# Setting the single_packet flag on SyncE's loads and stores in a rotary-embedding score kernel

## Chip, cores and metric

The kernel runs on one core of one Trainium2 chip. The metric is the device time of one execution in microseconds. A run counts as fast when it is within 1.5% of the fastest run of the same kernel.

## The reference

```python
batch, seq, heads, dim = 16, 512, 16, 64          # q, k float32, [batch, seq, heads, dim]
q_rot = concat([q1*cos - q2*sin, q1*sin + q2*cos])  # halves of dim; the same for k
scores = np.einsum('bshd,bthd->bsht', q_rot, k_rot)  # float32, [16, 512, 16, 512]
```

The inputs are 67 MB, the output is 268 MB. Per batch and head there is one product of 512 x 64 by 64 x 512.

## The kernel before: the parts that matter

Rows of the sequence are dealt to 128 partitions, four (C = 4) to each. VectorE applies the rotation, TensorE transposes and multiplies, ScalarE copies the scores from PSUM into one of three stage buffers of 32 KB per partition (16 heads x 512 x 4 bytes), and SyncE issues the store. Every load and store goes through SyncE's ring; only the two small tables (cos, sin) are issued by ScalarE. A ring is the queue of transfers of one issuing engine; in the profile q1 is SyncE's, q10 ScalarE's, q0 GpSimd's. "Row" means a contiguous piece of memory per partition: 32 KB in a full store, 16 KB in a batch load. The cuts below have comments added.

```python
stage_pool = ctx.enter_context(tc.tile_pool(name="stage", bufs=3))
...
def load(which, b):                       # 30 of these: 128 rows of 16 KB, 2 MB
    ...
    nc.sync.dma_start(t.rearrange("p c (h d) -> p c h d", h=H), dram[which][b])
...
def store(i, st):                         # 59 of these: 128 rows of 32 KB, 4 MB
    o = o_v[i // C, i % C]
    if i < NST - 1:
        nc.sync.dma_start(o, st)
        return
    h = H - 2                             # the last store, in three pieces
    nc.sync.dma_start(o[:, :h], st[:, :h])
    nc.sync.dma_start(o[:116, h:], st[:116, h:])
    nc.sync.dma_start(o[116:, h:], st[116:, h:])
...
def scores(i, p, st):
    ...                                   # matmuls into ps
    nc.scalar.copy(out=so, in_=si)        # L173: st <- ps
    if b == 0 and p % 2 == 1:             # 16 of these: 128 rows of 8 KB, 1 MB
        nc.sync.dma_start(o_v[0, c, :, G * i : G * (i + 1)], st[:, G * c : G * (c + 1)])
```

## Time and profile before

| | before |
|---|---|
| time, median of the first 3 runs | 800.30 us (800.18 to 802.09) |
| span of the profiled execution | 799.0 us |
| moved | 336.17 MB, mean 421 GB/s |
| DMA engines busy with SyncE's ring | 98.6% of the span |

### The profile page before, as it was taken

Reading aid. Unit: us, or ns where it says so; the run is one execution under the profiler, and the core shown is the slowest. Engines: PE = TensorE matmul, PEld = TensorE weight load, DVE = VectorE, ACT = ScalarE, POOL = GpSimd, SP = SyncE. Lnnn points to the kernel's source line nnn. Section 1 sums busy time; section 2 is a strip of 40 time slices with the busy share of each in tenths; the row PEclk is TensorE's granted clock in tenths of the full one; section 3 lists DMA queues with packets and bytes.
Section 4 is the critical chain, followed back from the end, with each engine's and each line's share of the span. In section 5 each row is a group of like instructions: output and inputs, shape, how many; then the busy total and the mean of one; then the engine's idle time right before and its main releaser. Section 6 shows DMA issues by size and latency. Waiting matters only on the chain.

```text
span 799.0 us, 7715 instructions
## 1 busy us (share of the span) xinstructions
PE 691.3 (87%) x3072; PEld 299.3 (37%) x3072; DVE 544.6 (68%) x516; ACT 561.2 (70%) x647; POOL 0.7 (0%) x6
## 2 busy tenths in 40 slices
PE   4989998997979979799797997979979799799970
PEld 2444443343434334343343443424434343344420
DVE  6999987676866768577585775857758478585300
ACT  3888886775857758577585775757757677578870
POOL 0000000000000000000000000000000000000000
PEclk9999999898998989889898898988989899899995
DMA  9999999999999999999999999999999999998995
GB/s 355 422 424 424 432 427 433 425 435 427 421 437 426 439 427 430 433 431 430 431 428 433 434 428 429 433 438 420 418 426 434 435 415 418 426 440 375 422 439 231
DMA packets 17844, 336.17 MB, mean 421 GB/s; under 512 B 1808, under 2 KB 3088, under 8 KB 4240
## 3 DMA queue, kind: packets, MB, share of 16 engines
q1 hardware_dynamic: 17520, 335.55, 98.6%
q8 instruction: 24, 0.39, 0.2%
q10 hardware_dynamic: 288, 0.13, 0.1%
q14 instruction: 12, 0.10, 0.0%
HBM read 67.24 MB, written 268.44 MB: 420 GB/s over the span
## 4 chain that ended last, share of the span: by engine, by line
DMA 50%; PE 40%; ACT 4%; DVE 3%; issue 1%; ACTq 0%; SPq 0%; DVEq 0%
DMA out_dram<-st 47%; PE ps L166 30%; PE bank L127 10%; ACT st L173 4%; DMA q_sb<-in_q_dram 2%; DVE part L106 1%; DMA early<-in_k_dram 1%; DVE q_sb L107 0%; DVE k_sb L107 0%; DVE k_sb L111 0%; DVE q_sb L111 0%; DVE early L107 0%; DVE kT_t L142 0%; ACTq L281 0%; DVE early L111 0%
## 5 line engine op out<-in xcount | busy, mean ns | idle before, releaser
L173 ACT COPY st<-ps 128x1024 f32<-128x1024 f32 x512 | 494.7, 1018 | 203.7 <-DMA out_dram<-st 105.6
L166 PE MATMUL ps<-kT_t,qT_t 64*128 64x512 f32 x2048 | 548.9, 654 | 71.0 <-ACT st L173 70.9
L166 PEld LDWEIGHTS ps<-kT_t,qT_t 64*128 64x128 f32 x2048 | 185.0, 197 | 261.7 <-issue 144.6
L142 DVE COPY qT_t<-bank 128x512 f32<-128x512 f32 x118 | 81.6, 691 | 203.8 <-PE bank L127 203.8
L127 PEld LDWEIGHTS bank<-ident,q_sb 128*128 128x128 f32 x480 | 55.6, 152 | 102.5 <-issue 99.1
L127 PE MATMUL bank<-ident,q_sb 128*128 128x128 f32 x480 | 86.9, 308 | 0.9 <-PE ps L166 0.9
L127 PEld LDWEIGHTS bank<-ident,k_sb 128*128 128x128 f32 x480 | 50.5, 141 | 95.4 <-issue 38.7
L127 PE MATMUL bank<-ident,k_sb 128*128 128x128 f32 x480 | 78.7, 287 | 1.6 <-DVE qT_t L142 1.2
L142 ACT COPY kT_t<-bank 128x512 f32<-128x512 f32 x122 | 72.5, 599 | 6.4 <-PE bank L127 6.4
L107 DVE TENSOR_TENSOR q_sb<-q_sb,cos_t 128x1024 f32<-128x1024 f32 x60 | 73.5, 1226 | 2.1
L111 DVE TENSOR_TENSOR k_sb<-k_sb,part 128x1024 f32<-128x1024 f32 x60 | 73.5, 1225 | 2.1
L107 DVE TENSOR_TENSOR k_sb<-k_sb,cos_t 128x1024 f32<-128x1024 f32 x60 | 73.5, 1225 | 2.0
L106 DVE TENSOR_TENSOR part<-q_sb,ss_t 128x1024 f32<-128x1024 f32 x60 | 73.5, 1225 | 2.0
L106 DVE TENSOR_TENSOR part<-k_sb,ss_t 128x1024 f32<-128x1024 f32 x60 | 73.0, 1216 | 0.1
L111 DVE TENSOR_TENSOR q_sb<-q_sb,part 128x1024 f32<-128x1024 f32 x60 | 73.0, 1216 | 0.0
L127 PE MATMUL bank<-ident,early 128*128 128x128 f32 x64 | 10.5, 316 | 12.5 <-DVE early L111 10.6
L127 PEld LDWEIGHTS bank<-ident,early 128*128 128x128 f32 x64 | 8.3, 161 | 17.5 <-issue 13.4
L106 DVE TENSOR_TENSOR part<-early,ss_t 128x1024 f32<-128x1024 f32 x8 | 9.8, 1223 | 5.9 <-DMA early<-in_k_dram 5.8
L111 DVE TENSOR_TENSOR early<-early,part 128x512 f32<-128x512 f32 x16 | 10.3, 687 | 0.2
L107 DVE TENSOR_TENSOR early<-early,cos_t 128x1024 f32<-128x1024 f32 x8 | 9.8, 1225 | 0.3
L142 ACT COPY qT_t<-bank 128x512 f32<-128x512 f32 x10 | 5.7, 617 | 3.2 <-PE bank L127 3.2
L142 DVE COPY kT_t<-bank 128x512 f32<-128x512 f32 x6 | 4.1, 685 | 0.3 <-PE bank L127 0.3
(9 smaller groups left out, 2.8 us busy)
## 6 DMA issues: line engine op xcount, KB each, us to landing
out_dram<-st SPq DMA_DIRECT2D x59, 4096.0 KB, 23.9
k_sb<-in_k_dram SPq DMA_DIRECT2D x15, 2048.0 KB, 26.9
q_sb<-in_q_dram SPq DMA_DIRECT2D x15, 2048.0 KB, 29.9
out_dram<-st SPq DMA_DIRECT2D x16, 1024.0 KB, 14.3
out_dram<-st SPq DMA_DIRECT2D x1, 3584.0 KB, 20.4
early<-in_k_dram SPq DMA_DIRECT2D x1, 1536.0 KB, 8.9
early<-in_q_dram SPq DMA_DIRECT2D x1, 1536.0 KB, 12.1
early<-in_k_dram SPq DMA_DIRECT2D x1, 512.0 KB
```

The costliest lines, as they stand in the source:

```text
L106: nc.vector.tensor_tensor(pv, xs, ss, op=mult)
L107: nc.vector.tensor_tensor(xc, xc, cs, op=mult)
L111: nc.vector.tensor_tensor(y, y, z, op=add)
L127: nc.tensor.transpose(bank[:, x, :], src, ident)
L142: copy(out=dst, in_=src)
L166: nc.tensor.matmul(out=po, lhsT=lhs[64 * r : 64 * r + 64, :], rhs=rh, start=True, stop=True)
L173: nc.scalar.copy(out=so, in_=si)
```

## The change

The intent: let the descriptors of a transfer travel as one packet, so that the DMA engines pay less per row. The flag is set on 110 of SyncE's 112 transfers (the two odd pieces of the last store and ScalarE's two tables stay without it).

```diff
-        nc.sync.dma_start(t.rearrange("p c (h d) -> p c h d", d=D), src)
+        nc.sync.dma_start(t.rearrange("p c (h d) -> p c h d", d=D), src, single_packet=True)
...
-        nc.sync.dma_start(t.rearrange("p c (h d) -> p c h d", h=H), dram[which][b])
+        nc.sync.dma_start(t.rearrange("p c (h d) -> p c h d", h=H), dram[which][b], single_packet=True)
...
-            nc.sync.dma_start(o, st)
+            nc.sync.dma_start(o, st, single_packet=True)
...
-        nc.sync.dma_start(o[:, :h], st[:, :h])
+        nc.sync.dma_start(o[:, :h], st[:, :h], single_packet=True)
...
-            nc.sync.dma_start(o_v[0, c, :, G * i : G * (i + 1)], st[:, G * c : G * (c + 1)])
+            nc.sync.dma_start(o_v[0, c, :, G * i : G * (i + 1)], st[:, G * c : G * (c + 1)], single_packet=True)
```

## The prediction

> **What bounds the kernel now.** The first view read is the page's second and third part, because the change touches only transfers: the DMA row of the forty slices, the packet line, and the queues.
>
> ```profile
> DMA  9999999999999999999999999999999999998995
> ...
> DMA packets 17844, 336.17 MB, mean 421 GB/s; under 512 B 1808, under 2 KB 3088, under 8 KB 4240
> ## 3 DMA queue, kind: packets, MB, share of 16 engines
> q1 hardware_dynamic: 17520, 335.55, 98.6%
> ...
> q10 hardware_dynamic: 288, 0.13, 0.1%
> ```
>
> The sixteen DMA engines are busy in 37 of 40 slices at the top digit and only dip in the last few. q1, SyncE's ring, holds 335.55 of 336.17 MB and keeps the engines busy for 98.6% of 799.0 us, which is 788 us. Only about 11 us of the whole span are not spent on that ring's packets. So the kernel is bound by moving bytes, and the question is how many bytes per ns an engine moves, not who waits. The only other ring that the kernel uses itself, q10 (the two ScalarE table loads), has 288 small packets.
>
> The second view is the busy time by stretches, here the 700 us between head and tail.
>
> ```profile
> core 0: us, PE busy (x) PEld busy (x) DVE busy (x) ACT busy (x) POOL busy (x), PEclk, DMA share, GB/s
> ...
> 20.00:720.00 700.00, 629.54 (x2809) 271.56 (x2807) 510.37 (x481) 507.49 (x587) 0.00 (x0) 0.93 1.00 429
> ```
>
> Over those 700 us the DMA share is 1.00 at 429 GB/s. TensorE is busy for 630 of 700 us, VectorE for 510, ScalarE for 507: none is full, and TensorE has about 10% of slack. The 429 GB/s is the rate of a saturated path.
>
> The third view is the group that links the engines to the transfers, and the DMA queue's own waits, to see whether issuing could bind.
>
> ```profile
> L173 ACT COPY st<-ps 128x1024 f32<-128x1024 f32 x512 | 494.7, 1018 | 203.7 <-DMA out_dram<-st 105.6
> ```
>
> ```profile
> SPq L147 <- ACT st L173: 657.0, 59, 16.6
> SPq L176 <- ACT st L173: 49.1, 16, 14.8
> SPq L281 <- DMA out_dram<-st: 17.6, 1, 17.6
> ```
>
> ```profile
> out_dram<-st SPq DMA_DIRECT2D x59, 4096.0 KB, 23.9
> k_sb<-in_k_dram SPq DMA_DIRECT2D x15, 2048.0 KB, 26.9
> q_sb<-in_q_dram SPq DMA_DIRECT2D x15, 2048.0 KB, 29.9
> ```
>
> ScalarE stands idle 105.6 us because the stage buffer that it must fill is still being stored. SyncE in turn stands 657 + 49 us waiting for ScalarE to fill it, so the sequencer that issues the transfers is nearly always idle. A 4096 KB store takes 4.19 MB / 432 GB/s = 9.7 us if it has the engines to itself; its median landing time is 23.9 us. The other 14 us are transfers queued ahead of it. That is the picture of a backlog at the engines.
>
> **How a packet costs its time.** The trace has a record for each packet. Nearly all the 32,768-byte ones on q1 took 1213 ns, the 16,384-byte ones 611 ns, the 8,192-byte ones 309 ns, the 3,072-byte ones 121 ns, the 1,024-byte ones 46 ns and the 4-byte semaphore writes 9 ns. From the first two: (1213 - 611) / 16,384 = 0.0367 ns per byte, and 611 - 602 = 9 ns fixed. The fit gives 46.6 ns at 1,024 bytes and 122 at 3,072, so it holds. One engine moves 32,768 / 1213 = 27.0 bytes per ns, sixteen move 432 GB/s. I also count: 59 stores of 128 rows, 30 loads of 128, 16 early stores of 128, four head loads of 512, and 256 rows in the split last store make 15,744. With 110 x 16 + 4 + 12 = 1776 semaphore writes that is 17,520, exactly the page's number. So in the kernel before, a packet record is one contiguous row, with nothing merged.
>
> **What the Trainium skill says.** No page of it names the flag. Three places bear on it, all in "DMA: Bandwidth & Descriptors". "SWDGE vs HWDGE vs iDMA" describes a packet, for the software (GpSimd) path, as "≤4096 B preferably, ≤64 descriptors", and says that transfers issued from SyncE and ScalarE take their descriptors from dedicated hardware and not from software. The largest flagged transfer here, by descriptors, is a head load: 512 rows over 16 engines, 32 each, under 64. The page shows q1 as hardware_dynamic, which agrees with the path; no run here shows the packet rule. "Why small descriptors are slow (HBM only)" gives a fixed cost of about 3 cycles per packet and calls packetization worth it only at 256 B or less. The trace agrees in kind, with 9 ns fixed per packet; this kernel's rows are 1 KB to 32 KB, where 9 ns is 20% to 0.7%, and nearly all bytes are in the large ones. "Where 436 GB/s comes from" puts the fabric's ceiling at 435.2 GB/s; the trace's 432 GB/s inside packets lies just under it. The same section's 358 GB/s for HBM traffic is not what binds here: the page has 421.
>
> **The change part by part.** It sets a flag on 110 of SyncE's 112 transfers; the last two (the 116- and 12-partition pieces of the final store) stay as they were. No transfer is added, removed, resized or moved, and the comparison of instruction order finds every engine the same, row by row. Then I built both kernels and compared what the compiler emits. The intermediate program differs in that one field on exactly those 110 copies, and in nothing else about a copy. The final instruction streams of all five engines, SyncE's included, are the same byte for byte: the field is dropped on the way for transfers issued from SyncE. The sum is therefore 110 x 0 ns = 0 us. What remains is the spread between executions: 800.18, 800.30 and 802.09 us before.
>
> **The rivals.** They matter only if the chip somehow sees the flag, for instance if the program is built otherwise there than here.
>
> First, packets merge and get cheaper. At most 15,744 - 128 = 15,616 rows become 110 x 16 = 1760 packets, which spares 13,856 x 9 ns / 16 engines = 7.8 us. With the engines as the bound all of it would count: 800.5 - 7.8 = 792.7 us, 1.0% faster. For it: the engines are full. Against it: the identical programs. Even so it stays within 2%, since the fixed part is so small at these row sizes.
>
> Second, coarser packets delay something. If an engine changes rings only between packets, the table loads on q10 would have to let whole head loads pass: 32 rows of 46 ns is 1.5 us for each of the first two. VectorE already waits 5.8 us for the first head load, so 1.5 to 3 us would be added at the start: about 803 us. In the body there is no second ring with work, so nothing can be delayed.
>
> Third, issuing gets dearer. The issues take 0.33 us for a store and up to 0.93 us for a load, and SyncE has over 700 us of idle time; only the six issues at the start follow one another without a wait (0.66, 0.60, 0.62, 0.63, 0.93, 0.42 us). Doubling them costs at most 3.9 us, 804 us.
>
> Fourth, a packet is read whole before it is written. A store's share per engine would be eight rows, 8 x 1213 ns = 9.7 us. If reading and writing stopped overlapping, the 788 us might nearly double. Nothing speaks for it except that I cannot rule it out without a run; it is the tail on the slow side.
>
> **Range and chances.** The centre is the kernel's own median, 800.3 us, moved up by 0.2 us as one of the three times lay 1.8 us above it: 800.5 us. Nothing in the change widens the spread, so the range covers the old spread and a little more for another chip or hour: 799.2 to 802.4 us. Faster by over 2% would need 16 us, twice what merging could give: 0.005. Slower by over 2% needs the fourth rival: 0.01. The rest, 0.985, is within 2%.
>
> **What would show it right or wrong.** Right: q1 still has 17,520 packets, 98.6% give or take 0.2, with 1213 and 611 ns for the two large sizes; the stretch from 20 to 720 us still shows 428 to 430 GB/s; a store still lands after about 24 us; store issues still take 0.33 us. Fewer packets on q1 would prove that the flag acts. The same number with another duration would mean that it acts inside an engine without changing the records. A later first VectorE product than 5.76 us would point to the second or third rival. A time below 796 or above 806 us, with the same packets and durations, would mean that the bound was misread.

## More of the kernel before

Verdicts use a threshold of 2%.

The prediction quotes the lines that carry the argument. To them belongs one more line of the page's first part, busy time and share of the span by engine:

```profile
PE 691.3 (87%) x3072; PEld 299.3 (37%) x3072; DVE 544.6 (68%) x516; ACT 561.2 (70%) x647; POOL 0.7 (0%) x6
```

No engine that computes is full; the sixteen DMA engines are.

## The result and the profile after

The time after is 800.88 us (median of 6 runs, 800.06 to 801.50), before it is 800.85 us (6 runs, 799.82 to 802.09). The ratio is 0.9999 with a 95% interval of 0.9986 to 1.0012: the same. Ratios here and below are the mean time of one kernel's fast runs over the mean time of the other's of the same rounds, so not quite the ratio of the medians beside them.

The page of the kernel after, engines and DMA rows, which answer to those of before:

```profile
PE 684.4 (86%) x3072; PEld 296.5 (37%) x3072; DVE 544.6 (68%) x516; ACT 561.4 (70%) x647; POOL 0.7 (0%) x6
...
DMA  9999999999999999999999999999999999998995
...
DMA packets 17844, 336.17 MB, mean 421 GB/s; under 512 B 1808, under 2 KB 3088, under 8 KB 4240
...
q1 hardware_dynamic: 17520, 335.55, 98.4%
```

The packet counts are equal to the last packet, in every size class. That is the line to read first: rows that became fewer and longer packets would show here, whatever that did to the time. What the profile counts as a packet is one row, however, so a grouping of rows that leaves their records as they are would not show in this count; against that speak the built programs, the times, and the turns between rings in gp4k_on below. The durations agree too: 1213, 611, 309, 121, 46 and 9 ns are the medians in both traces for the six sizes that the prediction lists.

The busy time by stretches of the kernel after (the columns are those of the prediction), then the group that links the engines to the transfers, its DMA queue's waits and its DMA issues:

```profile
20.00:720.00 700.00, 624.25 (x2812) 269.63 (x2811) 510.47 (x481) 508.08 (x588) 0.00 (x0) 0.94 1.00 429
```

```profile
L173 ACT COPY st<-ps 128x1024 f32<-128x1024 f32 x512 | 494.8, 1019 | 202.7 <-DMA out_dram<-st 118.1
```

```profile
SPq L147 <- ACT st L173: 657.4, 59, 16.5
SPq L176 <- ACT st L173: 49.9, 16, 15.2
```

```profile
out_dram<-st SPq DMA_DIRECT2D x59, 4096.0 KB, 25.1
k_sb<-in_k_dram SPq DMA_DIRECT2D x15, 2048.0 KB, 28.5
q_sb<-in_q_dram SPq DMA_DIRECT2D x15, 2048.0 KB, 27.6
```

Same share, same 429 GB/s, same waits of the queue within 1 us. What does differ shows how much two executions of the same instructions differ: the part of ScalarE's idle time that is put down to the stores by 12.5 us (105.6 and 118.1, while its whole idle time differs by 1), TensorE's busy time by 7 us (691.3 and 684.4, at a granted clock of 0.923 and 0.932) and the landing times by 1 to 2 us (23.9 and 25.1 for a store; loads up in one tensor, down in the other). Without the packet counts beside them, a reader could take any of these for an effect. One such difference even changes a name in the list of groups, before and then after:

```profile
L106 DVE TENSOR_TENSOR part<-early,ss_t 128x1024 f32<-128x1024 f32 x8 | 9.8, 1223 | 5.9 <-DMA early<-in_k_dram 5.8
```

```profile
L106 DVE TENSOR_TENSOR part<-early,ss_t 128x1024 f32<-128x1024 f32 x8 | 9.8, 1222 | 6.0 <-ACT ss_t L198 5.8
```

The first product on VectorE needs both the first load and a table that ScalarE prepares. They arrive close together. Before, the table was ready at 5.57 us and the product began at 5.76, with the load; after, the table was ready at 5.80 us and the product began at 5.84. Which came last varies: of the experiments below without GpSimd loads, four name ScalarE (two of them without the flag) and two name the load, both without the flag, at 5.6 to 6.3 us.

### The profile page after: what moved, and what is told of

The parts are those of the page before. It is cut to its first block, busy times and chain, and to the rows that moved or that the text cites. A ratio compares the mean times of both kernels' runs of the same rounds, so it can differ in the third digit from the quotient of the medians.

```text
span 799.2 us, 7715 instructions
## 1 busy us (share of the span) xinstructions
PE 684.4 (86%) x3072; PEld 296.5 (37%) x3072; DVE 544.6 (68%) x516; ACT 561.4 (70%) x647; POOL 0.7 (0%) x6
## 3 DMA queue, kind: packets, MB, share of 16 engines
q1 hardware_dynamic: 17520, 335.55, 98.4%
## 4 chain that ended last, share of the span: by engine, by line
DMA 50%; PE 36%; DVE 5%; ACT 5%; issue 1%; ACTq 0%
DMA out_dram<-st 49%; PE ps L166 27%; PE bank L127 9%; ACT st L173 5%; DVE part L106 2%; DVE early L111 1%; DVE k_sb L111 1%; DVE k_sb L107 1%; DVE early L107 1%; DMA sin_t<-in_sin_dram 1%; DVE kT_t L142 0%; DVE q_sb L107 0%; DVE q_sb L111 0%; ACTq L281 0%; DVE qT_t L142 0%
## 5 line engine op out<-in xcount | busy, mean ns | idle before, releaser
L173 ACT COPY st<-ps 128x1024 f32<-128x1024 f32 x512 | 494.8, 1019 | 202.7 <-DMA out_dram<-st 118.1
L166 PE MATMUL ps<-kT_t,qT_t 64*128 64x512 f32 x2048 | 541.9, 646 | 76.5 <-ACT st L173 76.4
L166 PEld LDWEIGHTS ps<-kT_t,qT_t 64*128 64x128 f32 x2048 | 182.2, 195 | 264.1 <-issue 135.9
## 6 DMA issues: line engine op xcount, KB each, us to landing
out_dram<-st SPq DMA_DIRECT2D x59, 4096.0 KB, 25.1
```

What stands on the lines that cost most here:

```text
L166: nc.tensor.matmul(out=po, lhsT=lhs[64 * r : 64 * r + 64, :], rhs=rh, start=True, stop=True)
```

## The experiments

The theory: the flag is dropped when the program is built, so that the chip never sees it. It rests on a comparison of the built programs: the instruction streams of the five engines are the same byte for byte. (The comparison does see edits: the run heads15 below changes 118 bytes of SyncE's stream. It gave the same five streams for before, after and all_on, for rows4k_off and rows4k_on, and for gp4k_off and gp4k_on.) The rival: the flag acts, but this kernel cannot show it, because its rows are large or because cheaper packets lie behind something else. The first four runs ask whether cheaper or dearer packets would show at all, and then look where there is much to merge. All runs are correct unless it is said otherwise.

### rows4k_off: many more packets, no flag

```diff
-            nc.sync.dma_start(o, st)
+            nc.sync.dma_start(o, st, max_dma_last_dim=4096)
```

> The kernel before, without the flag, with its 59 full stores cut into rows of 4 KB instead of 32 KB. The bytes are the same; q1 should show 17,520 + 59 x 896 = 70,384 packets. If the DMA engines bound the kernel and each packet has a fixed 9 ns: 59 x 896 x 9 ns / 16 = 29.7 us more, about 830 us; a 4 KB record should take 159 ns. Rival (packet costs hide behind waits, so that merging could never have shown in the time): about 801 us.

Measured: 823.57 us (4 runs, 822.85 to 824.70) against 800.90; ratio 1.0280 (1.0264 to 1.0296). The page and the body's stretch:

```profile
DMA packets 70708, 336.17 MB, mean 409 GB/s; under 512 B 1808, under 2 KB 3088, under 8 KB 64656
...
q1 hardware_dynamic: 70384, 335.55, 100.8%
```

```profile
20.00:720.00 700.00, 610.63 (x2740) 264.53 (x2738) 496.25 (x468) 496.03 (x574) 0.00 (x0) 0.92 1.02 414
```

The packets are counted as forecast and a 4 KB record takes 159 ns, yet 22.4 us came (between the means of the runs) where 29.7 were expected. The reason can be read in the share: 100.8%, more than all the time there is. Records of one engine overlap. The records do not name their engine, but from start to start the most frequent distances between records of one size are 1209 ns for 32 KB, 607 ns for 16 KB and 155 ns for 4 KB; the slope is the same 0.0367 ns per byte, but the fixed part is 607 - 602 = 5 ns and not 9. The record is 4 ns longer than the place it takes. With 5 ns, 52,864 more packets cost 52,864 x 5 / 16 = 16.5 us. In the same trace the loads' 16 KB records are longer on average, 666 against 626 ns: 3840 x 40 / 16 = 9.6 us. Together 26 us, nearer to the 22.4 but above it; the rest was not tested. All in all a further packet cost 22.4 x 16 / 52,864 = 6.8 ns here. The rival's case "nothing would show" has fallen: packet costs reach the time.

### rows4k_on: the same with the flag

```diff
-            nc.sync.dma_start(o, st, single_packet=True)
+            nc.sync.dma_start(o, st, max_dma_last_dim=4096, single_packet=True)
```

> The same 4 KB rows with the flag on the same 110 transfers. Theory (the flag never reaches the hardware on this ring): the time of the run without the flag, within 0.15%, 70,384 packets on q1, 159 ns each. Rival (the flag acts, but the kernel before leaves it only 1% to gain, and nothing came through): here up to 30 us are to be won, so fewer packets and a time near 800 to 810 us.

Measured: 821.68 us (5 runs, 820.79 to 825.39); ratio to before 1.0269 (1.0246 to 1.0292).

```profile
DMA packets 70708, 336.17 MB, mean 410 GB/s; under 512 B 1808, under 2 KB 3088, under 8 KB 64656
...
q1 hardware_dynamic: 70384, 335.55, 100.9%
```

```profile
20.00:720.00 700.00, 619.66 (x2735) 267.48 (x2734) 496.56 (x469) 496.05 (x573) 0.00 (x0) 0.92 1.02 414
```

Not one packet fewer, the same 159 ns and 155 ns, the same 414 GB/s, and the streams of the two kernels are again the same bytes. The medians are 1.9 us apart, a little more than the 0.15% that I had allowed (1.2 us), but the ranges lie in one another and the ratios' intervals overlap. Up to 22 us were to be won, and nothing came. Of the runs, this is the one that decides against a flag that acts unseen on this ring.

### all_on: the flag on all 114 transfers

```diff
-        nc.sync.dma_start(o[:116, h:], st[:116, h:])
-        nc.sync.dma_start(o[116:, h:], st[116:, h:])
+        nc.sync.dma_start(o[:116, h:], st[:116, h:], single_packet=True)
+        nc.sync.dma_start(o[116:, h:], st[116:, h:], single_packet=True)
 ...
-            nc.scalar.dma_start(t, src.rearrange("(p c) j -> p c j", c=C))
+            nc.scalar.dma_start(t, src.rearrange("(p c) j -> p c j", c=C), single_packet=True)
```

> The flag on all 114 transfers, those of ScalarE and the two odd-shaped last stores too. Theory: 800.9 us within 1 us, 17,520 packets on q1 and 288 on q10. Rival (the two last pieces were left out because the flag does something to them, at 29 rows per engine): a different tail, an end more than 1 us earlier or later.

Measured: 800.82 us (5 runs, 800.51 to 801.34) against 800.90, ratio 0.9995 (0.9982 to 1.0007); 17,520 packets on q1, 288 on q10. So no reason is seen here for leaving out the two pieces, and the flag does nothing on ScalarE's two transfers either.

### heads15: fewer bytes

```diff
-            nc.sync.dma_start(o, st)
+            nc.sync.dma_start(o[:, : H - 1], st[:, : H - 1])
```

> Wrong on purpose: the 59 full stores leave out the last of 16 heads, so the result is wrong and 15.5 MB fewer are moved; all compute stays. If the DMA engines are the bound: 15.47 MB / 432 GB/s = 35.8 us less, about 765 us, with TensorE at some 90% busy. Rival (TensorE or the waits set the pace, so that cheaper transfers could not have shown): above 790 us.

Measured: 765.18 us (4 runs, 764.87 to 765.74), ratio 0.9551 (0.9538 to 0.9564), result wrong as meant. The expectation was 765. The page and the body's stretch of this run:

```profile
PE 670.8 (88%) x3072; PEld 292.7 (38%) x3072; DVE 544.6 (71%) x516; ACT 560.7 (73%) x647; POOL 0.7 (0%) x6
...
q1 hardware_dynamic: 17520, 320.08, 98.6%
```

```profile
20.00:720.00 700.00, 642.64 (x2960) 279.99 (x2959) 528.54 (x500) 535.07 (x619) 0.00 (x0) 0.96 1.00 427
```

The same compute takes 35.7 us less, the bytes' share at 432 GB/s, and the engines are as full as before. So a saving at the DMA engines would have come through; that no saving showed after the change is no matter of hiding.

### gp4k_off and gp4k_on: the loads on GpSimd's ring, without and with the flag

Here the 30 batch loads leave SyncE's ring for the software one, in rows of 4 KB so that there is something to merge.

```diff
-        nc.sync.dma_start(t.rearrange("p c (h d) -> p c h d", h=H), dram[which][b])
+        nc.gpsimd.dma_start(t.rearrange("p c (h d) -> p c h d", h=H), dram[which][b], max_dma_last_dim=4096)
```

gp4k_on has `single_packet=True` as well.

> The 30 batch loads issued from GpSimd (software descriptors) instead of SyncE, in rows of 4 KB, without the flag: the reference for the next run. Their own queue should hold 15,360 data packets and the time should rise, by up to 11,520 x 5 to 9 ns / 16 = 4 to 7 us for the packets, or more if the second queue disturbs the stores.

> The same with the flag on those 30 loads[...]. The compiled streams of the two kernels are the same byte for byte, so by the theory (the flag is dropped when the program is built, on every ring) time and packet counts are those of the run without it, within 0.3%. Rival (the flag works on the software ring and only SyncE's ring ignores it): fewer or longer packets on GpSimd's queue, or a time that differs by more than 0.5%.

Measured: 851.86 us (4 runs, 851.62 to 854.71) without and 851.93 us (4 runs, 851.15 to 852.39) with the flag; ratios to before 1.0635 and 1.0627. Queue and issues without, then with the flag:

```profile
q0 software_dynamic: 15840, 62.92, 18.7%
...
k_sb<-in_k_dram POOLq DMA_DIRECT2D x15, 2048.0 KB, 34.1
q_sb<-in_q_dram POOLq DMA_DIRECT2D x15, 2048.0 KB, 40.2
```

```profile
q0 software_dynamic: 15840, 62.92, 18.7%
...
k_sb<-in_k_dram POOLq DMA_DIRECT2D x15, 2048.0 KB, 34.2
q_sb<-in_q_dram POOLq DMA_DIRECT2D x15, 2048.0 KB, 40.4
```

The flag does nothing here either, as the equal programs said; whether the hardware could make something of it stays open, since with this build it cannot be delivered. What I did not foresee is the 50 us that both pay; I had given 4 to 7 us, with a caveat about the stores. In the list of groups, first of the kernel before and then of gp4k_off, VectorE's first products on the k tiles now wait 154 us in all for their loads, where they hardly waited before:

```profile
L106 DVE TENSOR_TENSOR part<-k_sb,ss_t 128x1024 f32<-128x1024 f32 x60 | 73.0, 1216 | 0.1
```

```profile
L106 DVE TENSOR_TENSOR part<-k_sb,ss_t 128x1024 f32<-128x1024 f32 x60 | 73.0, 1217 | 154.2 <-DMA k_sb<-in_k_dram 154.1
```

The wait is passed on: TensorE's transposes of k stand 141 us for VectorE (1.2 us before), and between 20 and 720 us the DMA engines are busy for 0.95 of the time, at 395 GB/s, where it was 1.00 and 429. ScalarE, which stood 105.6 us for stores before, now stands 3.0 us for them. So the late loads have taken the place of the full engines as what holds the kernel up.

### gp_off: the same ring with 16 KB rows

The edit is that of gp4k_off without the row limit, and without the flag.

> The 30 batch loads issued from GpSimd, without the flag, with their whole 16 KB rows: asks why the run with 4 KB rows on that ring cost 50 us. If the engines take one packet from each ring in turn, a load of 4 KB rows has 32 packets per engine, each behind a store's row of 1.21 us: 32 x (1.21 + 0.16) = 44 us at worst (34 to 40 measured). With 16 KB rows it is 8 x (1.21 + 0.61) = 14.6 us, so the loads should land in 15 to 20 us and most of the 50 us should go: 800 to 810 us. If the software ring itself is slow, the loads still land after 30 us or more and the time stays near 850 us.

Measured: 819.53 us (4 runs, 816.79 to 822.33), ratio 1.0220 (1.0200 to 1.0239), just at the threshold: the verdict is unclear. Queue and issues, and the group of the head:

```profile
q0 software_dynamic: 4320, 62.92, 18.4%
...
k_sb<-in_k_dram POOLq DMA_DIRECT2D x15, 2048.0 KB, 21.3
q_sb<-in_q_dram POOLq DMA_DIRECT2D x15, 2048.0 KB, 21.0
```

```profile
L106 DVE TENSOR_TENSOR part<-early,ss_t 128x1024 f32<-128x1024 f32 x8 | 9.8, 1222 | 23.4 <-DMA early<-in_q_dram 16.8 <-ACT ss_t L198 6.4
```

The loads land after 21 us, a little over the 15 to 20 expected, and 32 of the 50 us are gone with no other edit than the row's length. This is what comes of engines that take one row from each ring in turn: a 4 KB row waits as long for its turn behind a 32 KB store row as a 16 KB row does, so it gets a quarter as much. The packet records show the turns (they do not name their engine, so a few of the pairs counted here are chance). In gp4k_off, 4,436 of the loads' rows start while at least 12 store rows of 32 KB are under way; 155 or 156 ns later, the distance that a 4 KB row takes, a store row starts in 3,877 cases and another 4 KB row in 62. In gp_off it is 952 and 21 of 1,124 rows (607 or 608 ns later). With the flag, in gp4k_on, it is 3,751 and 103 of 4,323, so the flag did not put a load's rows into one turn either. The Trainium skill, "DMA: Bandwidth & Descriptors", section "Queues, rings and completion order", has the engines go round between rings packet by packet; it calls 9 to 17 descriptors a typical packet. With packets of that length, a load's 8 or 32 rows per engine would have needed one to four turns, with rows of one load behind each other; here a turn is one row. Most of the remaining 18 us lies at the start, where my expectation of 800 to 810 us failed: VectorE now waits 23.4 us instead of 5.9 for the head's loads, 17.5 us more. The first batch loads no longer queue behind them on the same ring, and the two larger head loads land after 28.7 and 31.9 us instead of 8.9 and 12.1.

### tail and tail4: one engine ends late

In the traces of before and after, one DMA engine works on alone for the last 3 us or so, and is late by about 8 us against most others. Both runs shift part of the last store away from it, or try to.

```diff
-        h = H - 2
+        h = H - 6            # tail;  tail4: h = H - 4 and the pieces of 116 and 12 kept
 ...
-        nc.sync.dma_start(o[:116, h:], st[:116, h:])
-        nc.sync.dma_start(o[116:, h:], st[116:, h:])
+        nc.sync.dma_start(o[:119, h:], st[:119, h:])
+        nc.sync.dma_start(o[119:, h:], st[119:, h:])
```

> A byproduct, without the flag. In the traces of before and after one single DMA engine goes on for about 8 us when the others have ended. The last store is cut at 10 heads instead of 14, and its last 6 heads go as 119 partitions and 9 instead of 116 and 12, so that the late engine has 8 rows of 20 KB and one of 12 KB instead of 8 of 28 KB and one of 4 KB: 8 x 0.757 + 0.457 us = 6.5 us against 8.6 us. If 119 partitions run on seven engines and the late one is not among them: 2.1 us earlier, about 798.7 us. If it is among them, it has 17 rows of 0.457 us more: about 806 us.

> A byproduct, without the flag: the last store is cut at 12 heads instead of 14 and keeps the pieces of 116 and 12 partitions. The run with 119 partitions put the late engine among those that take the second piece; with 116 it was not among them. The late engine then has 8 rows of 24 KB and one of 8 KB, 8 x 0.908 + 0.306 = 7.6 us, against 8 x 1.059 + 0.155 = 8.6 us: about 1.1 us earlier, ratio 0.9987. The engines of the 116 rows end at about 797 us, just before it. If the late engine is another one than assumed: no gain, or up to 4 us more.

Measured, tail: 807.95 us (6 runs, 806.77 to 809.25) against 801.29, ratio 1.0078 (1.0061 to 1.0094): some 6 us slower, clear of the noise. The stretch near its end:

```profile
799.00:805.00 6.00, 0.00 (x0) 0.00 (x0) 0.00 (x0) 0.00 (x0) 0.00 (x0) 0.50 0.06 27
```

A share of 0.06 is one engine of sixteen, moving one engine's 27 GB/s, with 12 KB records: the late engine did get 17 rows more, the second branch of the expectation. By the Trainium skill, "DMA: Bandwidth & Descriptors", section "Why a DMA increments its semaphore by 16 and not by 1", a transfer from SyncE uses the largest number of engines up to 16 that divides the slowest dimension on both of its sides, here the partitions, and takes the lowest-numbered ones. Worked out from that, 119 partitions use the lowest 7 engines, 116 the lowest 4, 12 the lowest 12; the trace of before agrees with the numbers 4 and 12, as the prediction's count of 1776 semaphore writes shows. In the trace of before the late engine ends with one 4 KB piece, so it is among the 12 and not among the 4; by tail it is among the 7. That leaves three engines by the page's numbering, which the trace does not show. Measured, tail4: 800.18 us (5 runs, 799.91 to 801.94) against 801.40, ratio 0.9993 (0.9980 to 1.0007). The sign is the expected one, the interval holds both no gain and the 1.1 us. I call it unproven, so no version here beats the two kernels.

## Why the prediction was right

- **The bound.** Held: bytes through the DMA engines. heads15 shows that less DMA work is paid back in full (35.7 of 35.8 us), rows4k_off that more packets cost time. One reading is off without consequence: the DMA row has 38 of 40 slices at the top digit, not 37.
- **The sum, 110 x 0 ns.** Held: the centre was 800.5 us, the measured 800.88 us lies in the range; 17,520 packets with the forecast durations; the share fell by 0.2 points, the edge of what was allowed. After the equal streams, rows4k_on is the strongest evidence, since there a working flag would have had over 20 us to give.
- **First rival, merging.** It did not occur. Its size, 7.8 us, was too large: it took 9 ns per packet from the length of a record, but the record overlaps the next one. With the 5 ns from start to start it is 13,856 x 5 / 16 = 4.3 us, with the 6.8 ns of rows4k_off 5.9 us. The conclusion (within 2% even then) only gets firmer.
- **Second rival, a coarser packet delays the tables.** It did not occur: VectorE's first product started at 5.84 us. That is later than 5.76, which the prediction had named as a sign of this rival, but inside the spread of the other runs without GpSimd loads (5.62 to 6.25 us), so the sign was drawn too sharply.
- **Third rival, dearer issues.** It did not occur: stores are issued in 0.33 us as before.
- **Fourth rival, no overlap of reading and writing.** It did not occur: 1213 ns and 429 GB/s.
- **What stays open.** What the flag would do if it reached the hardware. No run could deliver it: in this build it vanishes on SyncE's, ScalarE's and GpSimd's rings.

## What to carry to other kernels

Before reasoning about what an option does to the hardware, compare the built programs with and without it: identical streams settle the matter, and one run that gives the option much to win (here four-kilobyte rows) confirms it. Then read counts and durations before times: equal ones mean that no rows became longer packets, whatever TensorE's busy time or a landing time does. On a kernel bound by DMA, look instead at bytes, at row length and at which ring carries what.

## What the Trainium skill lacked or had wrong

- No page names this flag, or says that an option of a transfer may be dropped when the program is built. Here it is on three rings (ratio 0.9999 on SyncE's; 851.86 and 851.93 us on GpSimd's). It belongs to "DMA: Bandwidth & Descriptors".
- The same page, "Why small descriptors are slow (HBM only)", gives a fixed cost of about 3 cycles per packet, with 32 B to a cycle, and calls packetization worth it only at 256 B or less. An estimate from it, with the 0.0367 ns per byte of the traces, is 3 x 32 x 0.0367 = 3.5 ns per row. The traces show 5 ns from start to start, and a further row cost 6.8 ns of engine time in all (22.4 us for 52,864 rows). So splitting 32 KB rows into 4 KB ones cost 2.8%, about twice what that estimate gives, at rows far above 256 B.
- The same page, "Where 436 GB/s comes from", says that the HBM side, about 358 GB/s, binds for such transfers. For one core alone the sentence misleads: here 429 GB/s were held over 700 us, with loads and stores mixed. The 425 GB/s that the same section mentions as measured fits.
- The same page, "Queues, rings and completion order", gives 9 to 17 descriptors as a typical packet between two turns. Here a turn was one row, whether of 4 KB or 16 KB (a store row next in 3,877 of 4,436 cases in gp4k_off and 952 of 1,124 in gp_off).
- No page says that the profile's records of consecutive rows on one engine overlap, so that a share can pass 100% (100.8% in rows4k_off); the same page says only that an engine's descriptors are pipelined.
